# A decoder block's MLP weights: steps of the first up units and of the second down chunk held back and pinned in order, the last sums of up laid between the first down products

## The chip, the cores and the metric

The kernel runs on one core of a Trainium2 chip. The metric is the device time of one execution in microseconds (us). TensorE is called PE below, VectorE DVE, ScalarE ACT, GpSimd POOL and SyncE SP, as the profile does.

## What is computed

A decoder block on a sequence of 1024 rows of 1024 numbers: two token mixers (dilated attention and retention) behind one input projection, an output projection with a residual add, and an MLP. The change touches the last two steps:

```python
x = x + y @ w_out[l]
xn2 = rmsnorm(x, norm2_g[l])
x = x + jnp.square(jax.nn.relu(xn2 @ w_up[l])) @ w_down[l]
```

`w_up` is 1024 x 4096, `w_down` 4096 x 1024, all in float32.

## The kernel before

**Products.** Every float32 operand is split into a high half (`h`, a rounded copy made by ACT, line 320) and a low half (`l`, the rest, a subtraction on DVE, line 321). A product is three matmuls: high by high, high by low, low by high. The matmuls stand in `Pipe.group`, line 223. The large projections, up and down among them, are done by a scheme with seven products in place of eight, named N1 to N7. For it sums and differences of weight quarters are made first.

**Weights.** The class `Weights` holds a list of steps. A step takes a weight quarter that SP has loaded into a buffer `raw`, makes a sum on DVE where the scheme needs one (line 121 for the units of up, line 153 for the chunks of down), and splits it. Steps run strictly in the order of the list. `pump` runs as many as can run: those whose place is free and whose raw buffers can be loaded. It is called whenever a place comes free, and loads the next raw buffers behind each step, so a step that is issued later also sends its loads to SP's queue later. For up a unit (16 of them) has the pieces A, D, B and C; the list starts A of unit 0, A of unit 1, then D, B and C of unit 0, and so on. For down a chunk (8 of them) has seven steps, N1, N2, N3, N5, N7, N6, N4, of which the last four need a sum. Chunks use two sets of places in turn; some of the second set's lie in buffers that only come free when up ends (`n2a`, `n3a`, `y1a`, `w1a` and others).

**Order of the instructions.** PE's order is as written. On the other engines a scheduler may move an instruction ahead of others by its own estimate of when the inputs are there. `keep_in_program_order(ins)` pins one instruction behind everything that was recorded before it on its engine.

**The end of the output projection, place one below.** For each of eight row tiles `t` DVE adds the residual (`xr`, line 1148), ACT squares it, DVE and POOL make the inverse root (`ssq`, lines 1152 and 333, 334), and DVE scales the two halves of the row (`xn2`, line 1156). PE transposes the result into a PSUM tile `tr` (line 1092; there are two such tiles), and `turn_xn` makes the operands of up from it: `x0`, `x2`, `x3` and, last, `x1` (line 1112), each with a split. The line 1112 row is the last reader of its `tr` tile.

**The end of up and the start of down, place two.** `result` squares the ReLU of up's products (`u3`, `u2`, `q11`, `q12`), makes four sums `s` from each unit (line 1197) and sends all of it to memory (`h_d`). Down reads its rows back from there (`load_rows`), splits them (`part_rows`: ACT line 1245, POOL line 1246), and runs its products `down(u, name)`, where a unit `u` is a chunk and one of four row tiles. The result of a product is added into the output rows `Y` by DVE (line 1279) or copied there by ACT (line 1277); N1 is copied by ACT with its sign turned (`ms`, line 1271). Two products of unit 0 run inside up's last unit, the others behind it.

Of the kernel before, what the change touches and what calls it, by code (L numbers as in the profile page):

```python
# [10 lines left out]
F = mybir.dt.float32  # L11
R = mybir.dt.float32r
AF = mybir.ActivationFunctionType
# [4 lines left out]
P = 128  # L18
# [19 lines left out]
class Weights:  # L38
# [12 lines left out]
    def __init__(self, nc, rawp, wp, split):  # L51
# [8 lines left out]

        self.places = {}

    def claim(self, buf, key):
# [31 lines left out]
    def add_units(self, tag, srcs):  # L95

        base = len(self.src)
        kept = {}
        for s in srcs:
# [3 lines left out]
        def piece(key, buf, r, cols, then=None):  # L103
            def step():
# [4 lines left out]
                else:  # L109
                    h, l = self.buffer(buf)  # L110
                self.split(h, l, self.raw[r][:, cols])
                self.units[key] = h, l
# [5 lines left out]
        def sums(r):  # L118
            (x22, x21), (x11, x12) = ((self.raw[i][:, 0:512], self.raw[i][:, 512:1024]) for i in (r, r + 1))
            for x, y in ((x22, x21), (x21, x11), (x11, x22), (x12, x11)):  # L120
                self.nc.vector.tensor_tensor(x, x, y, op=OP.add)

# [14 lines left out]
    def add_chunks(self, tag, srcs, buffers):  # L137


        for c, quarters in enumerate(srcs):  # L140
# [4 lines left out]
            for name, r, other, op, ends in (  # L145
# [4 lines left out]

                def step(r=r, other=other, op=op, ends=ends, buf=buf, key=key):
                    if other is not None:
                        self.nc.vector.tensor_tensor(self.raw[r], self.raw[r], self.raw[other], op=op)  # L153
                    h, l = self.buffer(buf)
                    self.split(h, l, self.raw[r])
                    self.units[key] = h, l
                    self.used.update(ends)
# [22 lines left out]
    def pump(self, most=99):  # L180
        while most > 0 and self.next < len(self.steps):
            before, r, step = self.steps[self.next]
# [69 lines left out]

DOWN = ("N6", "N5", "N7", "N3", "N4", "N1", "N2")
BANK = {"N1": "a", "N2": "a", "N6": "b", "N7": "b", "N4": "b", "N5": "d", "N3": "d"}

# [14 lines left out]
def hybrid_block(ctx: ExitStack, tc: tile.TileContext, a: dict, out: bass.AP):  # L270
# [47 lines left out]

    def split(dst_h, dst_l, src):
        nc.scalar.activation(dst_h, src, AF.Copy)  # L320
        nc.vector.tensor_tensor(dst_l, src, dst_h.bitcast(F), op=OP.subtract)  # L321
# [16 lines left out]


    W = Weights(nc, rawp, wp, split)  # L340
    heads = [(slot, g) for slot in range(SLOTS) for g in (1, 2, 0)]
    for slot, g in heads:
# [733 lines left out]
    with ExitStack() as ph:  # L1076
# [10 lines left out]
        def turn_xn(xn, t, q):  # L1087
# [25 lines left out]
            put(OP7["N4"], cut, x1)  # L1113

        order = [(0, t) for t in range(NT)] + [(1, t) for t in (0, 4, 1, 5, 2, 3, 6, 7)]
        ahead = []
# [14 lines left out]
        for nb in range(2):  # L1131
            us = W.take(4)
            ns = halves()[nb]
            for n, t in enumerate([t for b, t in order if b == nb]):
# [16 lines left out]
                if nb == 1:  # L1151
# [3 lines left out]
                    for q, (cs, x2) in enumerate(zip(halves(), (y0, y))):  # L1155
                        nc.vector.scalar_tensor_tensor(xn[:, cs], x2, ssq[:, t, 3:4], g2[:, cs],
                                                       op0=OP.mult, op1=OP.mult)
                        pipe.at(2 if n > 5 else 1, lambda xn=xn, t=t, q=q: turn_xn(xn, t, q))

    last_turn = max(pipe.due)  # L1160


    with ExitStack() as ph:
# [16 lines left out]
        def result(j, f, cs, src):  # L1180
# [19 lines left out]
        held = {}  # L1200

# [115 lines left out]
        W.free(("place", "y1"))  # L1317
        load_rows(3)


    with ExitStack() as ph:
# [117 lines left out]
```

## Time and profile before

| | |
|---|---|
| median of 3 runs | 2254.57 us (2253.41 to 2255.34) |
| profiled execution | 2252.05 us |
| its span | 2250.3 us |
| PE busy | 2211.8 us (98%) |
| DVE busy | 1351.1 us (60%) |
| ACT busy | 1047.8 us (47%) |
| POOL busy | 398.6 us (18%) |
| granted PE clock, mean | 0.998 |

A row of a timeline in the profile gives the start and the duration of one instruction in us, the engine, the line, the operation with its output and inputs and, in brackets, how long the engine had stood idle before it and what ended that. A row on weight halves has the line of the helper `split`, so it is told from others by its tile: `wh` and `wl` are weights, `xh` and `xl` operands (or weights that lie in an operand's buffer). Matmuls follow each other before the one in front has ended, so durations of neighbours overlap. The profile is of one execution; its matmul ends are modelled.

### The profile page before, as it was taken

Reading aid. Unit: us, or ns where it says so; the run is one execution under the profiler, and the core shown is the slowest. Engines: PE = TensorE matmul, PEld = TensorE weight load, DVE = VectorE, ACT = ScalarE, POOL = GpSimd, SP = SyncE. Lnnn points to the kernel's source line nnn. Section 1 sums busy time; section 2 is a strip of 40 time slices with the busy share of each in tenths; the row PEclk is TensorE's granted clock in tenths of the full one; section 3 lists DMA queues with packets and bytes.
Section 4 is the critical chain, followed back from the end, with each engine's and each line's share of the span. In section 5 each row is a group of like instructions: output and inputs, shape, how many; then the busy total and the mean of one; then the engine's idle time right before and its main releaser. Section 6 shows DMA issues by size and latency. Waiting matters only on the chain. (4 is left out here: it accounts for less than half of the span.)

```text
span 2250.3 us, 30678 instructions
## 1 busy us (share of the span) xinstructions
PE 2211.8 (98%) x10772; PEld 1893.1 (84%) x10772; DVE 1351.1 (60%) x2570; ACT 1047.8 (47%) x2352; POOL 398.6 (18%) x436
## 2 busy tenths in 40 slices
PE   8999999999999999999999999999999999899999
PEld 7999999998888888888888877787788888678787
DVE  6444545454644445557777767783855556777874
ACT  6444434445343333445555544442555555654542
POOL 1111111110000000001222130000000000587873
PEclk9999999999999999999999999999999999999999
DMA  4313222322233333253563477774244456644432
GB/s 150 99 50 102 72 83 86 104 86 94 71 113 113 113 113 113 103 175 102 151 193 112 127 244 266 264 240 160 102 140 150 150 152 203 222 149 172 174 126 103
DMA packets 247852, 311.64 MB, mean 138 GB/s; under 512 B 15377, under 2 KB 171409, under 8 KB 247698
## 3 DMA queue, kind: packets, MB, share of 16 engines
q1 hardware_dynamic: 247698, 309.69, 42.5%
q8 instruction: 84, 1.38, 0.2%
q14 instruction: 70, 0.57, 0.1%
HBM read 209.92 MB, written 99.71 MB: 138 GB/s over the span
## 5 line engine op out<-in xcount | busy, mean ns | idle before, releaser
L321 DVE TENSOR_TENSOR wl<-raw,wh 128x1024 fp32r<-128x1024 f32 (+2 forms) x290 | 317.4, 1097 | 366.5 <-ACT wh L320 365.4
L223 PE MATMUL mm<-wh,xh 128*128 128x384 f32 (+1 forms) x1226 | 482.0, 393 | 1.8 <-ACT xh L320 1.3
L223 PE MATMUL mm<-wh,xl 128*128 128x384 f32 (+1 forms) x1226 | 439.1, 358 | 2.3 <-DVE xl L321 2.2
L320 ACT ACTIVATE wh<-raw 128x1024 fp32r<-128x1024 f32 (+2 forms) x290 | 273.5, 945 | 360.3 <-PE ms L223 110.8
L223 PE MATMUL mm<-wl,xh 128*128 128x384 f32 (+1 forms) x1226 | 437.6, 357 | 0.0
L223 PE MATMUL mm<-xh,wh 128*128 128x512 f32 x720 | 281.6, 391 | 5.0 <-ACT ms L387 5.0
L223 PE MATMUL mm<-xl,wh 128*128 128x512 f32 x720 | 280.7, 390 | 1.7 <-DVE xl L321 1.7
L223 PE MATMUL mm<-xh,wl 128*128 128x512 f32 x720 | 280.7, 390 | 0.0
L223 PE MATMUL ms<-xh,wh 128*128 128x512 f32 x700 | 275.6, 394 | 1.9 <-DVE St L886 1.6
L223 PE MATMUL ms<-xl,wh 128*128 128x512 f32 x700 | 272.6, 389 | 0.0
L223 PE MATMUL ms<-xh,wl 128*128 128x512 f32 x700 | 272.5, 389 | 0.0
L223 PEld LDWEIGHTS mm<-wh,xl 128*128 128x128 f32 x1226 | 230.7, 188 | 23.0 <-DVE xl L321 3.7
L223 PEld LDWEIGHTS mm<-wh,xh 128*128 128x128 f32 x1226 | 231.8, 189 | 21.6 <-ACT xh L320 1.7
L223 PEld LDWEIGHTS mm<-wl,xh 128*128 128x128 f32 x1226 | 232.6, 190 | 16.7
L223 PEld LDWEIGHTS mm<-xh,wh 128*128 128x128 f32 x720 | 135.6, 188 | 35.1 <-ACT ms L387 7.1
L223 PEld LDWEIGHTS mm<-xl,wh 128*128 128x128 f32 x720 | 135.5, 188 | 30.1 <-DVE xl L321 2.1
L223 PEld LDWEIGHTS mm<-xh,wl 128*128 128x128 f32 x720 | 135.5, 188 | 28.1
L223 PEld LDWEIGHTS ms<-xh,wh 128*128 128x128 f32 x700 | 131.5, 188 | 30.3 <-DVE St L886 2.0
L223 PEld LDWEIGHTS ms<-xh,wl 128*128 128x128 f32 x700 | 131.4, 188 | 27.4
L223 PEld LDWEIGHTS ms<-xl,wh 128*128 128x128 f32 x700 | 131.5, 188 | 26.3
L334 POOL TENSOR_TENSOR ssa<-ssa,half 128x2 f32<-128x2 f32 x96 | 66.5, 693 | 427.3 <-DVE ssa L333 410.3
L872 POOL TENSOR_TENSOR st<-st,half 128x1 f32<-128x1 f32 x32 | 27.5, 858 | 645.3 <-DVE st L871 645.2
(300 smaller groups left out, 3663.6 us busy)
## 6 DMA issues: line engine op xcount, KB each, us to landing
raw<-in_w_att SPq DMA_DIRECT2D x48, 384.0 KB, 3.9
raw<-in_w_up SPq DMA_DIRECT2D x32, 512.0 KB, 4.0
h_d<-s SPq DMA_DIRECT2D x64, 256.0 KB, 4.5
raw<-in_w_down SPq DMA_DIRECT2D x32, 512.0 KB, 4.4
s<-sg_d SPq DMA_DIRECT2D x40, 256.0 KB, 4.0
xh<-h_d SPq DMA_DIRECT2D x11, 896.0 KB, 4.5
s<-on_d SPq DMA_DIRECT2D x36, 256.0 KB, 5.0
xl<-h_d SPq DMA_DIRECT2D x10, 896.0 KB, 4.7
```

Of the source, the lines that this page charges most:

```text
L223: self.nc.tensor.matmul(ps, x, y, start=start, stop=stop, skip_group_check=not first)
L320: nc.scalar.activation(dst_h, src, AF.Copy)
L321: nc.vector.tensor_tensor(dst_l, src, dst_h.bitcast(F), op=OP.subtract)
L334: nc.gpsimd.tensor_tensor(dst, dst, half[:, :w], op=OP.pow)
L872: nc.gpsimd.tensor_tensor(st[:, 9:10], st[:, 8:9], half[:, 0:1], op=OP.pow)
```

## The change

Four edits. The first holds back the list of weight steps: a `limit` stops `pump` behind the first two steps of up while the output projection runs, and behind the first chunk of down while up runs; each limit is lifted later (the first behind the output projection, the second when the first down unit is issued). The second pins the sums and the high halves (ACT's copies) of the held-back steps, D, B and C of up's units 0 and 1 and the whole second chunk of down, behind what was recorded before them. The third records the four last sums `s` of up one by one (`add_tail`), the last unit's pinned and laid between the first seven down products. The fourth takes these seven products out of the last loop and records them ahead of it, so that the second chunk's steps come behind them in the program. No arithmetic or transfer is added or removed, and PE's order stays as it was.

```diff
     def pump(self, most=99):
-        while most > 0 and self.next < len(self.steps):
+        while most > 0 and self.next < len(self.steps) and self.next != self.limit:
...
-                self.split(h, l, self.raw[r][:, cols])
+                self.split(h, l, self.raw[r][:, cols], key[0] == "up" and key[1] < 2 and key[2] != "A")
...
-                self.nc.vector.tensor_tensor(x, x, y, op=OP.add)
+                ins = self.nc.vector.tensor_tensor(x, x, y, op=OP.add)
+                if tag == "up" and r <= base + 2:
+                    self.keep(ins)
...
-                def step(r=r, other=other, op=op, ends=ends, buf=buf, key=key):
+                def step(r=r, other=other, op=op, ends=ends, buf=buf, key=key, pin=c == 1):
                     if other is not None:
-                        self.nc.vector.tensor_tensor(self.raw[r], self.raw[r], self.raw[other], op=op)
+                        ins = self.nc.vector.tensor_tensor(self.raw[r], self.raw[r], self.raw[other], op=op)
+                        if pin:
+                            self.keep(ins)
                     h, l = self.buffer(buf)
-                    self.split(h, l, self.raw[r])
+                    self.split(h, l, self.raw[r], pin)
...
+DOWN_ORDER = (("N6", False), ("N5", False), ("N1", True), ("N7", False), ("N2", True), ("N3", False), ("N4", False))
...
-    def split(dst_h, dst_l, src):
-        nc.scalar.activation(dst_h, src, AF.Copy)
+    def split(dst_h, dst_l, src, pin=False):
+        hi = nc.scalar.activation(dst_h, src, AF.Copy)
+        if pin:
+            tc.keep_in_program_order(hi)
         nc.vector.tensor_tensor(dst_l, src, dst_h.bitcast(F), op=OP.subtract)
...
+        W.limit = W.first["up"] + 2
         order = [(0, t) for t in range(NT)] + [(1, t) for t in (0, 4, 1, 5, 2, 3, 6, 7)]
...
+    W.limit = None
+    W.pump()
     last_turn = max(pipe.due)
...
                 for name, x, y in (("N5", "u3", "u2"), ("N7", "u2", "q11"), ("N6", "q11", "N5"), ("N3", "q12", "N6")):
-                    held[j, name] = temps().tile([P, 512], F, name="s", bufs=4)
-                    nc.vector.tensor_tensor(held[j, name], held[j, x], held[j, y], op=OP.add)
-                    put_operand(j, name, held[j, name])
+                    tail.append((j, name, x, y))
+                    if j < NU - 1:
+                        add_tail()
...
+        def add_tail():
+
+            j, name, x, y = tail.pop(0)
+            held[j, name] = temps().tile([P, 512], F, name="s", bufs=4)
+            ins = nc.vector.tensor_tensor(held[j, name], held[j, x], held[j, y], op=OP.add)
+            if j == NU - 1:
+                tc.keep_in_program_order(ins)
+            put_operand(j, name, held[j, name])
...
+        W.limit = len(W.steps) - 7 * (NC - 1)
         stream = [(0, "N1"), (0, "N2")]
...
         W.free(("place", "y1"))
         load_rows(3)
+        for name, later in DOWN_ORDER:
+            down(later, name)
+            if name in ("N2", "N3", "N4"):
+                add_tail()
+        add_tail()
+        W.limit = None
...
-        for u in range(len(units)):
-            for name, later in (("N6", False), ("N5", False), ("N1", True), ("N7", False), ("N2", True),
-                                ("N3", False), ("N4", False)):
+        for u in range(1, len(units)):
+            for name, later in DOWN_ORDER:
```

Place one, DVE, in the kernel before: the norm of a row tile (`xr`, `ssq`, `xn2`) with the D pieces and the sums of up's units between its rows.

```order
L1148 TENSOR_TENSOR xr_15176<-mm_15244,xr_15176 128x512
L321 TENSOR_TENSOR wl4_15304<-raw0_14883,wh4_15303 128x512
L1152 TENSOR_TENSOR ssq_14655<-ssq_14655 128x1
L121 TENSOR_TENSOR raw0_14883<-raw0_14883 128x512
L333 TENSOR_SCALAR ssq_14655<-ssq_14655 128x1
L321 TENSOR_TENSOR wl4_15304<-raw2_14897,wh4_15303 128x512
L1156 SCALAR_TENSOR_TENSOR xn2_15293<-y0_15178,ssq_14655,g2_14653 128x512
L1156 SCALAR_TENSOR_TENSOR xn2_15293<-xr_15176,ssq_14655,g2_14653 128x512
L121 TENSOR_TENSOR raw0_14883<-raw0_14883,raw1_14895 128x512
L321 TENSOR_TENSOR xl_97<-x0_15319,xh_96 128x4x128
L121 TENSOR_TENSOR raw1_14895<-raw1_14895,raw0_14883 128x512
```

The same stretch of DVE in the changed kernel: from the row behind the same residual add to the first held-back row.

```order
L1163 TENSOR_TENSOR ssq_14655<-ssq_14655 128x1
L342 TENSOR_SCALAR ssq_14655<-ssq_14655 128x1
L1167 SCALAR_TENSOR_TENSOR xn2_15293<-y0_15178,ssq_14655,g2_14653 128x512
L1167 SCALAR_TENSOR_TENSOR xn2_15293<-xr_15176,ssq_14655,g2_14653 128x512
L330 TENSOR_TENSOR xl_97<-x0_15311,xh_96 128x4x128
L330 TENSOR_TENSOR xl_99<-x1_15329,xh_98 128x4x128
L1159 TENSOR_TENSOR xr_15240<-mm_15296,xr_15240 128x512
L1163 TENSOR_TENSOR ssq_14655<-ssq_14655 128x1
L342 TENSOR_SCALAR ssq_14655<-ssq_14655 128x1
L1167 SCALAR_TENSOR_TENSOR xn2_15345<-y0_15242,ssq_14655,g2_14653 128x512
L1167 SCALAR_TENSOR_TENSOR xn2_15345<-xr_15240,ssq_14655,g2_14653 128x512
L330 TENSOR_TENSOR wl4_15349<-raw0_14883,wh4_15348 128x512
```

The two norms now stand without weight rows between theirs; the first held-back row, `wl4`, comes behind the second.

Further on DVE, in the kernel before: from the first split of row tile 6's second half to its `x1` row.

```order
L321 TENSOR_TENSOR xl_93<-tr_15401,xh_92 128x4x128
L1107 TENSOR_TENSOR x2_15395<-x2_15395,tr_15401 128x512
L1108 TENSOR_TENSOR tr_15401<-x0_15259,tr_15401 128x512
L321 TENSOR_TENSOR xl_95<-x0_15259,xh_94 128x4x128
L321 TENSOR_TENSOR xl_13058<-x2_15395,xh_13057 128x4x128
L321 TENSOR_TENSOR xl_13062<-tr_15401,xh_13061 128x4x128
L1112 TENSOR_TENSOR x1_15277<-x1_15277,tr_15401 128x512
```

And in the changed kernel, from the first sums of unit 0 to the same `x1` row.

```order
L1113 TENSOR_TENSOR x0_15259<-x0_15259,tr_15390 128x512
L123 TENSOR_TENSOR raw1_14895<-raw1_14895,raw0_14883 128x512
L330 TENSOR_TENSOR xl_93<-tr_15401,xh_92 128x4x128
L123 TENSOR_TENSOR raw1_14895<-raw1_14895 128x512
L1117 TENSOR_TENSOR x2_15395<-x2_15395,tr_15401 128x512
L1118 TENSOR_TENSOR tr_15401<-x0_15259,tr_15401 128x512
L330 TENSOR_TENSOR wl2_15357<-raw1_14895,wh2_15356 128x1024
L330 TENSOR_TENSOR wl5_15361<-raw0_14883,wh5_15360 128x1024
L330 TENSOR_TENSOR xl_13062<-tr_15401,xh_13061 128x4x128
L330 TENSOR_TENSOR xl_95<-x0_15259,xh_94 128x4x128
L330 TENSOR_TENSOR xl_13058<-x2_15395,xh_13057 128x4x128
L1122 TENSOR_TENSOR x1_15277<-x1_15277,tr_15401 128x512
```

The sums and the two low halves of 1024 (pieces B and C of unit 0, `wl2` and `wl5`) now stand ahead of the `x1` row's last three splits; before, they stood ahead of the whole piece.

Place two, DVE, in the kernel before: from the first low half of the second chunk (`y1al`) to the eviction of unit 0's N7 (`Y4` with `ms`). `xl_93` is a weight's place here.

```order
L153 TENSOR_TENSOR raw0_17674<-raw0_17674,raw3_17710 128x1024
L401 TENSOR_TENSOR u2_17625<-mm_17627,u2_17625 128x512
L321 TENSOR_TENSOR xl_93<-raw2_17708,xh_92 128x1024
L321 TENSOR_TENSOR wl3_17769<-raw0_17674,wh3_17768 128x1024
L153 TENSOR_TENSOR raw3_17710<-raw3_17710,raw2_17708 128x1024
L1197 TENSOR_TENSOR s_17736<-u3_17663,u2_17625 128x512
L1197 TENSOR_TENSOR s_17739<-u2_17625,q11_17552 128x512
L1197 TENSOR_TENSOR s_17742<-q11_17552,s_17736 128x512
L321 TENSOR_TENSOR xl_93<-raw1_17706,xh_92 128x1024
L1197 TENSOR_TENSOR s_17745<-q12_17697,s_17742 128x512
L153 TENSOR_TENSOR raw2_17708<-raw2_17708,raw0_17674 128x1024
L1279 TENSOR_TENSOR Y4_15468<-Y4_15468,ms_17683 128x512
```

And in the changed kernel, from the last subtraction of up on.

```order
L411 TENSOR_TENSOR u2_17625<-mm_17627,u2_17625 128x512
L1302 TENSOR_TENSOR Y4_15468<-Y4_15468,ms_17683 128x512
L1219 TENSOR_TENSOR s_17798<-u3_17663,u2_17625 128x512
L1302 TENSOR_TENSOR Y0_15467<-Y0_15467,mm_17761 128x512
L1219 TENSOR_TENSOR s_17811<-u2_17625,q11_17552 128x512
L1219 TENSOR_TENSOR s_17823<-q11_17552,s_17798 128x512
L1219 TENSOR_TENSOR s_17826<-q12_17697,s_17823 128x512
L330 TENSOR_TENSOR y1al_17744<-raw0_17674,y1ah_17743 128x1024
L330 TENSOR_TENSOR xl_93<-raw1_17706,xh_92 128x1024
L330 TENSOR_TENSOR xl_93<-raw2_17708,xh_92 128x1024
L157 TENSOR_TENSOR raw0_17674<-raw0_17674,raw3_17710 128x1024
L1302 TENSOR_TENSOR Y5_17741<-Y5_17741,ms_17778 128x512
```

The eviction of N7 moved from behind the second chunk's first three low halves, three of its sums and all `s` to the row behind `u2`; the `s` rows stand next to it, and the second chunk behind them.

Place two, ACT, in the kernel before: the copies of the second chunk's last three steps and the eviction of unit 2's N1 (`ms`) behind them.

```order
L1277 ACTIVATE Y4_15468<-ms_17683 128x512
L1245 ACTIVATE xh_94<-r2_17754 128x256
L1277 ACTIVATE Y1_17752<-ms_17831 128x512
L320 ACTIVATE w1ah_17777<-raw3_17710 128x1024
L320 ACTIVATE w1bh_17779<-raw2_17708 128x1024
L320 ACTIVATE w1ch_17781<-raw1_17706 128x1024
L1277 ACTIVATE Y5_17753<-mm_17881 128x512
L1271 ACTIVATE ms_17898<-mm_17891 128x512
```

And in the changed kernel, where the same copies stand further on.

```order
L1300 ACTIVATE Y5_17741<-ms_17778 128x512
L327 ACTIVATE w1ah_17833<-raw3_17710 128x1024
L1300 ACTIVATE Y2_17747<-ms_17898 128x512
L1268 ACTIVATE xh_94<-xh_96 128x256 x2
L1300 ACTIVATE Y6_17748<-mm_17948 128x512
L1268 ACTIVATE xh_94<-xh_96 128x256
L327 ACTIVATE w1bh_17835<-raw2_17708 128x1024
L1294 ACTIVATE ms_17965<-mm_17958 128x512
```

The copy `w1bh`, pinned, now stands right in front of the eviction of unit 3's N1, with other evictions and row splits between the copies.

More of the change, by code (lines that the diff above doesn't have):

```diff
@@ L61, in __init__ @@
         self.places = {}
+        self.limit, self.keep, self.first = None, None, {}
     def claim(self, buf, key):
@@ L97, in add_units @@
         base = len(self.src)
+        self.first[tag] = len(self.steps)
         kept = {}
@@ L340, in hybrid_block @@
     W = Weights(nc, rawp, wp, split)
+    W.keep = tc.keep_in_program_order
     heads = [(slot, g) for slot in range(SLOTS) for g in (1, 2, 0)]
@@ L1195, in result @@
                 for name, x, y in (("N5", "u3", "u2"), ("N7", "u2", "q11"), ("N6", "q11", "N5"), ("N3", "q12", "N6")):
-                    held[j, name] = temps().tile([P, 512], F, name="s", bufs=4)
-                    nc.vector.tensor_tensor(held[j, name], held[j, x], held[j, y], op=OP.add)
-                    put_operand(j, name, held[j, name])
-        held = {}
+                    tail.append((j, name, x, y))
+                    if j < NU - 1:
+                        add_tail()
+        held, tail = {}, []
+        def add_tail():
[5 more added lines that the diff above has]
+            put_operand(j, name, held[j, name])
         def put_operand(j, name, x):
```

## The prediction

> **What bounds the kernel now.** I read the page first, then the waits of TensorE (PE), then a table of 25 us windows, then the timelines of the two windows in which PE loses most. The page:
>
> ```profile
> span 2250.3 us, 30678 instructions
> PE 2211.8 (98%) x10772; PEld 1893.1 (84%) x10772; DVE 1351.1 (60%) x2570; ACT 1047.8 (47%) x2352; POOL 398.6 (18%) x436
> ```
>
> PE is busy for 2211.8 of 2250.3 us, so 38.5 us is all that an edit can win which leaves its matmuls alone. The waits of PE from 1500 us on (line waited for: total, times, longest) and the windows (span, then busy time of PE, PEld, DVE, ACT, POOL, then the granted clock) show where the share of these two places lies:
>
> ```profile
> PE ms L223 <- DVE Y L1279: 5.8, 2, 5.0
> PE tr L1092 <- DVE x L1112: 2.8, 1, 2.8
> PE mm L223 <- ACT ms L1271: 1.4, 2, 0.9
> 1600.00:1625.00 25.00, 21.12 (x105) 16.57 (x103) 23.78 (x43) 15.92 (x29) 2.40 (x3) 1.00 0.30 101
> 1625.00:1650.00 25.00, 24.09 (x102) 20.01 (x103) 15.73 (x23) 15.32 (x25) 0.00 (x0) 0.93 0.28 84
> 1925.00:1950.00 25.00, 18.99 (x75) 14.58 (x74) 17.85 (x18) 15.91 (x29) 11.28 (x10) 0.93 0.80 277
> 1950.00:1975.00 25.00, 24.45 (x108) 19.93 (x107) 15.31 (x15) 18.55 (x38) 17.95 (x18) 1.00 0.40 139
> ```
>
> Place one is the start of up (1600 to 1630 us): VectorE (DVE) is busy for 23.78 of 25 us and PE waits for it. Place two is the end of up and the start of down (1930 to 1955 us). At both the granted clock averages 0.93 for a window: 0.07 x 25 = 1.75 us lost once more in each. PE at place one, and behind it PE at place two (start, duration, what, idle before):
>
> ```profile
> 1614.14 0.50 PE L223 MATMUL mm<-xl,wh 128*128 128x512 f32 x1 [1.73 <-DVE xl L321]
> 1622.69 0.40 PE L223 MATMUL mm<-xh,wl 128*128 128x512 f32 x1
> 1625.90 1.06 PE L1092 MATMUL tr<-ident,xn 128*128 128x128 f32 x4 [2.82 <-DVE x L1112]
> 1627.19 0.63 PE L223 MATMUL mm<-xl,wh 128*128 128x512 f32 x1
> 1629.58 0.39 PE L223 MATMUL mm<-xl,wh 128*128 128x512 f32 x1
> ...
> 1933.66 0.50 PE L223 MATMUL ms<-xh 128*128 128x512 f32 x1 [0.86 <-ACT Y L1277]
> 1938.11 0.39 PE L223 MATMUL mm<-wh,xl 128*128 128x512 f32 x1
> 1943.52 0.79 PE L223 MATMUL ms<-wh,xh 128*128 128x512 f32 x1 [5.02 <-DVE Y L1279]
> 1952.69 0.50 PE L223 MATMUL mm<-wh,rh 128*128 128x512 f32 x1 [0.55 <-ACT ms L1271]
> ```
>
> Behind each long wait the matmuls take 0.63 us in place of 0.39; at place one that ends by 1629.58, some 3.4 us after the wait. The wait of 5.02 us is for an eviction, Y -= PSUM of the first down unit's N7, which DVE does only at 1942.79 (row below). N7 started at 1933.66 and its six matmuls, 0.23 us apart, were done by about 1935.3: DVE was 7.5 us late, with weight steps of the second chunk in front.
>
> **Place one, step by step.** DVE's rows, by which the new order is added up:
>
> ```profile
> 1594.18 0.68 DVE L1148 TENSOR_TENSOR xr<-mm,xr 128x512 f32<-128x512 f32 x1
> 1596.66 0.75 DVE L1156 SCALAR_TENSOR_TENSOR xn<-y,ssq,g 128x512 f32<-128x512 f32 x1 [0.66 <-POOL ssq L334]
> 1598.00 0.68 DVE L1103 TENSOR_TENSOR x<-x,tr 128x512 f32<-128x512 f32 x1
> 1608.13 0.69 DVE L1148 TENSOR_TENSOR xr<-mm,xr 128x512 f32<-128x512 f32 x1
> 1615.81 1.22 DVE L321 TENSOR_TENSOR wl<-raw,wh 128x1024 fp32r<-128x1024 f32 x1
> 1616.94 0.69 DVE L1148 TENSOR_TENSOR xr<-mm,xr 128x512 f32<-128x512 f32 x1
> 1624.48 0.68 DVE L321 TENSOR_TENSOR xl<-tr,xh 128x512 fp32r<-128x512 f32 x1
> 1625.08 0.67 DVE L1112 TENSOR_TENSOR x<-x,tr 128x512 f32<-128x512 f32 x1
> 1649.08 0.69 DVE L121 TENSOR_TENSOR raw<-raw 128x512 f32<-128x512 f32 x1
> 1649.81 0.69 DVE L121 TENSOR_TENSOR raw<-raw,raw 128x512 f32<-128x512 f32 x1
> ```
>
> A 512-wide row starts 0.60 us after the one before it (1624.48 to 1625.08), a 1024-wide one takes 1.13 (1615.81 to 1616.94), a sum that waits for its predecessor 0.73 (1649.08 to 1649.81). A row norm with nothing else in it costs DVE 3.82 us, from the residual add at 1594.18 to 1598.00, of which it waits some 1.4 us for ACT and for GpSimd (POOL). In the kernel before, the last two norms (from 1608.13 and 1616.94) have weight rows laid into these holes. In the changed order the weight rows stand behind the last norm, so the holes are empty.
>
> From the common row at 1608.13 to the end of the L1112 row that PE waits for, the new order is: a norm 3.82, two low halves 1.20, a norm 3.82, which is 1616.97; then a D half and the first two sums, 0.73 + 0.73 + 0.60 to the next row; six rows of 512 (two of them sums) 3.60; two weight low halves of 1024 that now stand in front, 2.26; three low halves 1.80; the row itself 0.67. That ends at 1627.4, against 1625.08 + 0.67 = 1625.75: **+1.6 us**. The wait of 1.73 at 1614.14 shrinks, since the low half that ends it has one or two weight rows fewer ahead, but PE then only stands earlier at the 2.82 wait, which grows to about 6. It is worth nothing: DVE sets the end. A bound below is that DVE hides half of the holes (0.2 us later than before); above, that ACT's pinned copies hold DVE up by one copy more (+2.7).
>
> The slow clock goes the other way. If the slow stretch stands in time as it did (1625.9 to 1629.3), PE runs only 1.9 us of it and loses 0.9 in place of 1.75: **-0.8 us** (from 0 to -1.75). Last, the third 1024-wide weight row stands between the last rows' low halves, and the first N6 product needs one of those: up to one such row, 0 to 1.13, taken as **+0.6**. Place one: +1.6 - 0.8 + 0.6 = +1.4 us.
>
> [...]
>
> **Place two.** In the new order the N7 eviction stands right behind the u2 subtraction of the last up unit, ahead of all seven chunk-two splits and four sums; the last four up sums stand between the evictions. Waits of 0.86 and 5.02, the slow stretch of 1.75 and the 0.55 go: -8.2 us. What is late next are the held-back steps themselves, which now fall on the first down products:
>
> ```profile
> 1930.29 1.23 DVE L153 TENSOR_TENSOR raw<-raw,raw 128x1024 f32<-128x1024 f32 x1
> 1940.62 2.83 POOL L1246 TENSOR_TENSOR xl<-r,xh 128x256 fp32r<-128x256 f32 x2
> 1941.13 1.74 DVE L153 TENSOR_TENSOR raw<-raw,raw 128x1024 f32<-128x1024 f32 x1
> 1942.79 0.68 DVE L1279 TENSOR_TENSOR Y<-Y,ms 128x512 f32<-128x512 f32 x1
> 1946.61 0.73 POOL L1246 TENSOR_TENSOR xl<-r,xh 128x256 fp32r<-128x256 f32 x1 [3.16 <-ACT xh L1245]
> 1948.72 1.05 ACT L320 ACTIVATE w1ah<-raw 128x1024 fp32r<-128x1024 f32 x1
> 1952.05 0.59 ACT L1271 ACTIVATE ms<-mm 128x512 f32<-128x512 f32 x1
> raw<-in_w_down SPq DMA_DIRECT2D x32, 512.0 KB, 4.4
> ```
>
> For the weights themselves there is room. Eleven DVE rows at 1.74 are 19.1 us from about 1940 on, and their products (unit 4 on, three units of seven products of 1.36 us, six matmuls 0.23 us apart, behind unit 0) begin some 28 us after it. But ACT's queue is in order, and the pinned copies stand in it ahead of N1 evictions (L1271) on which PE waits for a PSUM bank. The copy w1bh waits for a sum that DVE makes behind another split: between 0 and one slowed sum and its copy, 1.74 + 1.05 = 2.8; I take 1.6, near to the slowed sum, since POOL is at work there. A copy of chunk three waits for its transfer, issued later than before because SP holds it behind DVE's pinned rows: between 0 and a whole landing of 4.4; I take 1.4, a third of it. With 0.2 for N1's eviction of unit 1 the new waits are **+3.2**, and place two is -8.2 + 3.2 = -5.0 us. No wait of these is over 2 us, so no slow stretch is counted.
>
> The same row shows two prices: 1.23 alone, 1.74 with POOL at work, and two POOL rows take 2.83 beside it where one takes 0.73 alone. [...] It speaks against the change, which moves eleven such rows to where POOL works; the sum has them at 1.74 already.
>
> **The sum.** The profiled execution took 2252.05 us (its span and 1.75 around it): 2252.05 + 1.4 - 5.0 = 2248.45. That execution lies 2.52 under the median of the runs, 2254.57; the same -3.6 from there gives **2251.0 us**, 0.16% less. About 0.2%, 4.5 us, is what a measurement of this kernel can tell from no change, so this counts as the same. With the new waits of place two between 0 and 2.8 + 4.4 its own range is 2248 to 2255.
>
> **Rivals.** First, the new waits do not come: ACT has its sums and landings in time, since DVE is busy for only 15.31 of 25 us from 1950 us on. Then -3.6 - 3.0 = -6.6, 2248.0, faster. For it: ACT is busy for 18.55 of 25 us at most here. Against: 0.55 of such a wait is there already.
>
> Second, slower: ACT is held at each of its seven pinned copies by a slowed sum, with an eviction behind each: 7 x 1.74 = 12.2 in place of 3.0, so -3.6 + 9.2 = +5.6, 2260.2. It decides from the point where more than half of the copies, about 6.6 us of holding, keep PE. Against it: three of the seven need no sum.
>
> [...]
>
> Fourth, the change does not do what it says: the N7 eviction stays late because ACT hands it over late. Place two then gains nothing and place one stands: +1.4, 2256.0.
>
> **Chances.** Forecast 0.55, first rival 0.22, second 0.06, third 0.13, fourth 0.04. Faster by over 0.2% (under 2250.1): the first and 0.06 of the forecast's own spread, 0.28. Slower by over 0.2%: the second and 0.02 of others, 0.08. The same: 0.64. The range, 2247.3 to 2256.0, reaches from the first rival to the fourth and leaves out the second.
>
> **What would show it.** Right: at place one PE's wait for the L1112 row (its new line) is 5 to 6.5 us, and the wait for xl before it under 1; at place two no wait for Y over 1 us, the clock at 1.00, and two waits of 1 to 2 us for the N1 eviction within 30 us. Wrong: a wait for L1112 under 4 us (the holes were filled after all), a wait for Y over 2 us, or ACT waits of over 4 us in all.

## The result and the profile after

The changed kernel took 2251.28 us (median of 22 runs, 2249.09 to 2254.3) beside 2254.66 of the kernel before: a ratio of 0.9986, 95% interval 0.9979 to 0.9992, so 3.2 us less (1.8 to 4.7). The forecast was 2251.0 and -3.6. Its profiled execution, however, took 2252.3 us, no less than the 2252.05 of the profile before. The page of the kernel after, span and busy times:

```profile
span 2250.5 us, 30672 instructions
PE 2212.8 (98%) x10772; PEld 1892.7 (84%) x10772; DVE 1352.6 (60%) x2570; ACT 1047.7 (47%) x2352; POOL 398.7 (18%) x436
```

The waits of TensorE (PE) from 1500 us on in the kernel after (line waited for: total, times, longest; L1122 and L1302 are the old L1112 and L1279, L1294 the old L1271):

```profile
PE tr L1102 <- DVE x L1122: 5.9, 1, 5.9
PE mm L229 <- ACT ms L1294: 4.1, 3, 1.9
PE ms L229 <- DVE Y L1302: 0.7, 1, 0.7
PE mm L229 <- DVE xl L330: 0.6, 2, 0.3
```

At the start of up the wait of 2.8 us has become one of 5.9, and the one of 1.73 ahead of it is down to 0.3; at the start of down the 5.0 us wait for Y is gone, and of the three waits for the N1 eviction two are new. The 25 us windows of the kernel after (span, then busy time of PE, PEld, DVE, ACT, POOL, then the granted clock):

```profile
1600.00:1625.00 25.00, 22.37 (x110) 17.57 (x108) 20.85 (x38) 15.30 (x28) 2.03 (x3) 1.00 0.21 73
1625.00:1650.00 25.00, 21.25 (x87) 17.60 (x88) 17.86 (x26) 14.57 (x25) 0.00 (x0) 0.86 0.31 91
1925.00:1950.00 25.00, 24.93 (x109) 20.27 (x110) 15.98 (x17) 17.76 (x35) 13.33 (x15) 1.00 0.82 270
1950.00:1975.00 25.00, 21.55 (x86) 16.74 (x85) 20.83 (x18) 17.20 (x33) 19.71 (x17) 0.93 0.50 170
```

DVE is now idle for 4 of 25 us in the window in which it sets the end (20.85, before 23.78): the empty holes of the norms. The clock reads 0.86 at place one (before 0.93), and the 0.93 of place two has moved from the first of its windows to the second. PE's timeline after, place one and place two (start, duration, what, idle before):

```profile
1613.90 0.50 PE L229 MATMUL mm<-xl,wh 128*128 128x512 f32 x1 [0.27 <-DVE xl L330]
1628.75 1.09 PE L1102 MATMUL tr<-ident,xn 128*128 128x128 f32 x4 [5.86 <-DVE x L1122]
1630.06 0.63 PE L229 MATMUL mm<-xl,wh 128*128 128x512 f32 x1
1633.30 0.39 PE L229 MATMUL mm<-xh,wh 128*128 128x512 f32 x1
...
1958.47 0.50 PE L229 MATMUL mm<-wh,rh 128*128 128x512 f32 x1 [1.55 <-ACT ms L1294]
1970.48 0.50 PE L229 MATMUL mm<-xh 128*128 128x512 f32 x1 [1.86 <-ACT ms L1294]
1971.52 0.63 PE L229 MATMUL mm<-xh 128*128 128x512 f32 x1
1982.63 0.50 PE L229 MATMUL mm<-xh 128*128 128x512 f32 x1 [0.73 <-ACT ms L1294]
```

The matmuls of 0.63 us are those at half clock. The wait of 1.86 us brought them on as well. The clock record of the traces gives the half-clock stretches as 3.413 us long (from 1625.94 and from 1943.38 us in the kernel before, from 1970.99 us in the kernel after) or twice that (6.827 us from 1626.25 us in the kernel after); 3.41 us is called a window of the clock below.

Where the time went is read from the same four matmuls in both traces, one ahead of and one behind each place (PE does the same matmuls in the same order in both). In the kernel before:

```profile
1590.07 0.39 PE L223 MATMUL mm<-wl,xh 128*128 128x512 f32 x1
1640.01 0.39 PE L223 MATMUL ms<-xh,wl 128*128 128x512 f32 x1
1925.17 0.39 PE L223 MATMUL mm<-wh,rh 128*128 128x512 f32 x1
1990.06 0.39 PE L223 MATMUL mm<-y1ah,xh 128*128 128x512 f32 x1
```

and in the kernel after:

```profile
1591.28 0.39 PE L229 MATMUL mm<-wl,xh 128*128 128x512 f32 x1
1643.29 0.39 PE L229 MATMUL ms<-xh,wl 128*128 128x512 f32 x1
1928.52 0.39 PE L229 MATMUL mm<-wh,rh 128*128 128x512 f32 x1
1990.24 0.39 PE L229 MATMUL mm<-y1ah,xh 128*128 128x512 f32 x1
```

Place one took 52.01 us in place of 49.94: +2.1. Place two took 61.72 in place of 64.89: -3.2. The 1.2 us ahead of 1591 lie ahead of the rows that the change moves. In six profiles of the experiments that leave place one as it was, the same stretch reads -0.5 to +5.4 us, so it is scatter between executions. With it the profile comes out even. The rest of the difference between profile and timed runs is the clock. The granted clock is listed for every run: its mean is 0.99720 over the 65 runs of the kernel before beside the experiments and 0.99764 over the 22 of the kernel after. Times the span of 2250 us that is 6.3 and 5.3 us lost. The two profiled executions lost 4.3 (half of 3.41 + 3.41 + 1.71 us at half clock, the last of them behind the last matmul) and 5.9 (half of 6.83 + 3.41 + 1.65). By this the profile before was lucky by 2.0 us and that after unlucky by 0.6, which is 2.6 of the 3.6 us by which the difference of the profiles (+0.25) and that of the medians (-3.4) disagree. It is an estimate that takes all clock lost for time lost, which after_fill below shows not to hold at place one.

### The profile page after: what moved, and what is told of

Same layout as the page of the kernel before. It is cut to its first block, busy times and chain, and to the rows that moved or that the text cites. A ratio compares the mean times of both kernels' runs of the same rounds, so it can differ in the third digit from the quotient of the medians.

```text
span 2250.5 us, 30672 instructions
## 1 busy us (share of the span) xinstructions
PE 2212.8 (98%) x10772; PEld 1892.7 (84%) x10772; DVE 1352.6 (60%) x2570; ACT 1047.7 (47%) x2352; POOL 398.7 (18%) x436
## 3 DMA queue, kind: packets, MB, share of 16 engines
q8 instruction: 84, 1.38, 0.2%
```

## The experiments

The table has, for every kernel, place one and place two against the kernel before, read from the same four matmuls; the stretches at half clock in each (us); and the ratio of the timed runs to those of the kernel before on the same chip, with its interval and in us of 2254.57. The readings of a place scatter: place two is unchanged in p1_only and p1_hold and reads -0.6 and +0.9, and p2_nopin and nopin_again are the same kernel.

| kernel | place one | place two | half clock one / two | ratio (95%) | us |
|---|---|---|---|---|---|
| changed kernel | +2.1 | -3.2 | 6.83 / 3.41 | 0.9986 (0.9979 to 0.9992) | -3.2 |
| p1_only | +1.9 | -0.6 | 6.83 / 3.41 | 1.0013 (1.0004 to 1.0022) | +2.9 |
| p2_only | -0.3 | -4.6 | 0 / 0 | 0.9976 (0.9966 to 0.9987) | -5.4 |
| p2_spread | -0.3 | -5.1 | 0 / 0 | 0.9970 (0.9960 to 0.9981) | -6.8 |
| after_fill | +1.7 | -2.1 | 0 / 3.41 | 0.9989 (0.9980 to 0.9998) | -2.5 |
| p1_hold | +0.3 | +0.9 | 0 / 6.83 | 0.9994 (0.9985 to 1.0003) | -1.4 |
| p2_nopin | -0.3 | -6.4 | 0 / 0 | 0.9962 (0.9948 to 0.9975) | -8.6 |
| p2_nosums | 0.0 | -4.2 | 3.41 / 0 | 0.9974 (0.9964 to 0.9985) | -5.9 |
| p2_late | 0.0 | -4.6 | 3.41 / 3.41 | 0.9968 (0.9956 to 0.9981) | -7.2 |
| pool_a | +1.9 | -6.2 | 6.83 / 0 | 0.9966 (0.9954 to 0.9978) | -7.7 |
| pool_b | +8.0 | -6.2 | 13.65 / 0 | 0.9998 (0.9990 to 1.0007) | -0.5 |
| pool_c | +5.8 | -6.6 | 10.24 / 0 | 0.9987 (0.9977 to 0.9996) | -2.9 |
| nopin_again | 0.0 | -6.8 | 3.41 / 0 | 0.9962 (0.9949 to 0.9974) | -8.6 |

**The two places apart.** p1_only has the edits of the start of up alone, p2_only those of the end of up and the start of down alone.

```diff
 p1_only, from the changed kernel
-    def step(..., key=key, pin=c == 1):
+    def step(..., key=key, pin=False):
...
-                    if j < NU - 1:
-                        add_tail()
+                    add_tail()
...
-            if j == NU - 1:
-                tc.keep_in_program_order(ins)
...
-        W.limit = len(W.steps) - 7 * (NC - 1)
...
-        for name, later in DOWN_ORDER:
-            down(later, name)
...
-        for u in range(1, len(units)):
+        for u in range(len(units)):
 p2_only, from the changed kernel
-        W.limit = W.first["up"] + 2
...
-                if tag == "up" and r <= base + 2:
-                    self.keep(ins)
-                self.split(h, l, self.raw[r][:, cols], key[0] == "up" and ...)
+                self.split(h, l, self.raw[r][:, cols])
```

> Place one alone: the hold and the pins at the start of up stay, the end of up and the start of down are as before the change. By the terms of the forecast: 1.4 us slower than the kernel before (1.6 of DVE order, 0.8 of slow clock less, 0.6 of wait for xl). By what the profile after the change shows, where TensorE stands 2.1 us later behind place one and the slow clock lasts for 6.83 us in place of 3.41: 2.1 us slower, and the wait for the L1122 row about 5.9 us again. Rival: the difference upstream of up (1.2 us in the profile at 1550 us) belongs to the change: 3.3 us slower.

> Place two alone: the start of up is as before the change, the weight steps of the second down chunk are held back and pinned and the last sums of up laid between the first down products. By the terms of the forecast: 5.0 us faster than the kernel before. By what the profile after the change shows (3.2 us won between 1890 and 1990 us, since a wait of 1.86 us brought a slow stretch of 3.41 us): 3.2 us faster. Rival: the two places are not independent, since place one shifts the phase at which the clock windows fall: then this and place one alone don't add up to the whole (0.9986 of the time before, 3.4 us).

PE's timeline in p1_only: the wait for L1122 is that of the changed kernel, and the long wait for Y of the kernel before is back (4.19 us, there 5.02).

```profile
1628.29 1.09 PE L1102 MATMUL tr<-ident,xn 128*128 128x128 f32 x4 [5.90 <-DVE x L1122]
1945.70 0.50 PE L229 MATMUL ms<-wh,xh 128*128 128x512 f32 x1 [4.19 <-DVE Y L1298]
```

PE's timeline in p2_only: the two waits for the N1 eviction.

```profile
1958.56 0.50 PE L227 MATMUL mm<-wh,rh 128*128 128x512 f32 x1 [1.54 <-ACT ms L1291]
1970.25 0.50 PE L227 MATMUL mm<-xh 128*128 128x512 f32 x1 [1.53 <-ACT ms L1291]
```

Place one alone costs 2.9 us (0.9 to 5.0), an interval that holds the 1.4, the 2.1 and the 3.3 of its expectation (the profile reads +1.9 at the place), and place two alone gains 5.4 (2.9 to 7.7); their sum, -2.5, is that of the whole (-3.2, 1.8 to 4.7) within the intervals. The changed kernel is a gain and a loss, as forecast. In p2_only the two waits, 1.54 and 1.53, brought no slow stretch, and place two gained 4.6 in place of 3.2.

**Is it the clock or DVE that costs at place one?** after_fill keeps PE busy through the long wait.

```diff
 after_fill, from the changed kernel
+        self.ps = ps
...
-    const.tile([P, 224], F, name="rest")
+    zero = const.tile([P, 224], R, name="rest")
+    nc.gpsimd.memset(zero.bitcast(F), 0.0)
...
             pt = tr.tile([P, 4, P], F, name="tr")
+            if (q, t) == (1, NT - 1):
+                for _ in range(48):
+                    nc.tensor.matmul(pipe.ps[:, :224], zero[:, :P], zero, start=False, stop=False, ...)
```

> The changed kernel, with 48 products of zeros (128x224, some 0.1 us each, 4.8 us in all) added into the open sum just ahead of the transposes that wait 5.86 us at place one; the result of the sum is unchanged. TensorE is then idle for about 1 us in place of 5.86, and the transposes start when they did. If the slow clock behind the wait is brought by the idle time and costs what its stretch of 6.83 us in the profile says, this is up to 3.4 us faster than the changed kernel; if it is one window in most runs, 1.7 us faster. Rival: the slow stretch hides beside DVE's work, which stays the bound behind place one: no difference, or slower by what the fill overruns.

PE's timeline in after_fill:

```profile
1623.70 5.51 PE L1104 MATMUL mm<-rest 128*128 128x224 f32 x48
1629.77 0.63 PE L1107 MATMUL tr<-ident,xn 128*128 128x128 f32 x4 [0.56 <-DVE x L1127]
1634.32 0.50 PE L230 MATMUL ms<-xh,wh 128*128 128x512 f32 x1 [0.48 <-ACT xh L328]
1635.42 0.51 PE L230 MATMUL ms<-xl,wh 128*128 128x512 f32 x1 [0.60 <-DVE xl L331]
```

The fill took the idle time and the slow stretch away (transposes of 0.63 us in place of 1.09, clock 1.00), and the time did not move: 0.9989 against 0.9986, each with runs of the kernel before beside it. By the two intervals the fill won some 1.8 us at most, which excludes the 3.4 and leaves one window's 1.7 at the edge. PE gained speed until 1634 and then waited 0.48 and 0.60 us for the operands of N6, which the changed kernel does not wait for there. So at place one the whole slow stretch of 6.83 us is worth 0.4 us (+1.7 in place of +2.1), not 3.4: it lies beside DVE's and ACT's next rows. The kernels without the change at place one say the same: with one slow stretch of 3.41 us they take 0.0 there, without one -0.3. PE in p2_only, p2_spread and p2_nopin, which have none, waits 0.67 us for an xl near 1633 us, and does not in p2_late, p2_nosums and nopin_again, which have one. The rival held.

**Hold or pins, at place one.** p1_hold keeps the limit and drops the pins.

```diff
 p1_hold, from p1_only
-                if tag == "up" and r <= base + 2:
-                    self.keep(ins)
-                self.split(h, l, self.raw[r][:, cols], key[0] == "up" and ...)
+                self.split(h, l, self.raw[r][:, cols])
```

> Place one alone, with the hold of the first two up units' steps, but without the pins on their sums and copies; place two as before the change. If the pins make the 2 us of place one, since without them the scheduler lays the weight rows into the holes of the last norms again, this is within 0.7 us of the kernel before, and the wait for the L1122 row is 3 us or less. If the hold itself makes them: 2 us slower than before, with a wait near 5.9 us.

PE's timeline in p1_hold:

```profile
1627.92 0.63 PE L1100 MATMUL tr<-ident,xn 128*128 128x128 f32 x4 [2.94 <-DVE x L1120]
```

The wait is 2.94 again and the time that of before (0.9994). Without pins the scheduler lays the weight rows into the holes again, and the hold by itself costs little: the place reads +0.3 with no slow stretch, where kernels with neither hold nor slow stretch read -0.3. The pins make the rest of the 1.9 us of p1_only.

**The parts of place two.** p2_nopin drops the pins on the held steps, p2_nosums the laying of the four sums.

```diff
 p2_nopin, from p2_only
-    def step(..., key=key, pin=c == 1):
+    def step(..., key=key, pin=False):
 p2_nosums, from p2_only
-                    if j < NU - 1:
-                        add_tail()
+                    add_tail()
...
-            if j == NU - 1:
-                tc.keep_in_program_order(ins)
...
-            if name in ("N2", "N3", "N4"):
-                add_tail()
-        add_tail()
```

> Place two alone, with the hold and the last four sums laid between the first down products, but without the pins on the second chunk's copies and sums. If the pins are what keeps VectorE free for the N7 eviction, the weight steps stand ahead of it again, a wait of 3 to 5 us for Y comes back and the gain falls from 5.4 to 2 us or less. If the hold and the sums do it: 5 us faster than before as with the pins, and the two waits for the N1 eviction (1.54 and 1.53 us) go, since the copies need not stand in front of it.

> Place two alone, with the hold and the pins, but the last four sums of up made at once, as before the change. If the laying of the sums matters, four sums of 0.7 to 1.0 us stand ahead of the evictions of the first down unit: a wait of 1 to 3 us for Y comes back, and this is 1 to 3 us slower than place two alone. Rival: within 0.5 us of place two alone, since the held-back weight steps were all the delay.

> p2_nopin again, as it was, beside the three variants on the same chip. It should come out at 0.9962 of the time before again, within 0.0013, if the gain over place two with pins (0.9976) is real; if that was the phase of the slow clock, at 0.997 to 0.998.

PE's timeline in p2_nopin, then ACT's:

```profile
1937.36 0.50 PE L227 MATMUL ms<-xh 128*128 128x512 f32 x1 [0.79 <-ACT Y L1297]
1940.59 0.50 PE L227 MATMUL mm<-wh,xh 128*128 128x512 f32 x1 [1.58 <-ACT ms L1291]
```

```profile
1949.24 0.58 ACT L1291 ACTIVATE ms<-mm 128x512 f32<-128x512 f32 x1
1950.60 1.04 ACT L325 ACTIVATE w1ah<-raw 128x1024 fp32r<-128x1024 f32 x1
1951.55 1.04 ACT L325 ACTIVATE w1bh<-raw 128x1024 fp32r<-128x1024 f32 x1
1952.50 1.04 ACT L325 ACTIVATE w1ch<-raw 128x1024 fp32r<-128x1024 f32 x1
```

Without pins no wait for Y came back. The three copies into w1 now stand in a row behind the N1 eviction of unit 2, none of them waiting, and the waits ahead of the N1 evictions of units 3 and 4 are gone. Left are 0.79 and 1.58 at the very start of down, the latter for unit 1's N1, and 0.87 us near 1980, which the kernel before has too. Place two gains 6.4 and 6.8 us in two profiles against 4.6 with pins, and the ratio is 0.9962 twice against 0.9976. The intervals of the ratios still overlap (0.9948 to 0.9975 and 0.9966 to 0.9987), so the 3 us between them are likely rather than certain. It has the lowest ratio of the study, though the intervals of p2_late and pool_a overlap with its own. p2_nosums is as fast as p2_only (0.9974 and 0.9976; no wait for Y over 0.3 us): the laying of the sums is worth nothing measurable. What p2_nopin and p2_nosums share is the hold, with the first unit's products recorded ahead of the held steps, and this is the likeliest to clear the way for the evictions. It is not shown alone: no run drops the pins and the laying together, or has one of these two edits without the other.

**Releasing the steps one at a time.** p2_spread releases one step behind each product of the second unit, p2_late the last three of them two to four products later.

```diff
 p2_spread, from p2_only
-        W.limit = len(W.steps) - 7 * (NC - 1)
+        HELD = W.limit = len(W.steps) - 7 * (NC - 1)
...
-        W.limit = None
...
                     down(u + later, name)
+                    if u < 3 and W.limit is not None and W.limit < HELD + 7:
+                        W.limit += 1
+                        W.pump()
...
 p2_late, the same with a table
+RELEASE = {(1, "N6"): 1, (1, "N5"): 1, (1, "N1"): 1, (1, "N7"): 1, (1, "N4"): 1, (2, "N1"): 1, (2, "N7"): 1}
```

> Place two alone, and the seven steps of the second down chunk released one behind each product of the second down unit, in place of all at once behind the first unit. If the two waits for the N1 eviction (1.55 and 1.86 us after the change) come from the pinned copies that stand in front of it in ACT's queue, they shrink to under 0.5 us each and no slow stretch follows: 3 to 5 us faster than place two alone. Rival: the waits are only moved, since chunk three's transfers are then issued later still: within 1 us of place two alone, with a wait of 1 to 2 us elsewhere between 1950 and 1990 us.

> Place two alone, the steps released one at a time as in p2_spread, but the last three later: one behind the second unit's N4, one behind the third unit's N1 and one behind its N7, so that the copy w1bh stands behind the N1 eviction that waited for it. If the order of ACT's queue makes the wait that is left (1.59 us), it goes and this is 1 to 1.5 us faster than p2_spread. Rival: VectorE's sums and splits of these steps, at 1.7 us each beside GpSimd, now stand ahead of Y evictions two units later, or chunk three's transfers come later: as p2_spread or up to 2 us slower, with the waits for Y (1.03 and 0.65 us) longer.

PE's timeline in p2_spread:

```profile
1957.29 0.50 PE L227 MATMUL mm<-wh,rh 128*128 128x512 f32 x1 [1.59 <-ACT ms L1291]
1961.34 0.50 PE L227 MATMUL ms<-wh,rh 128*128 128x512 f32 x1 [1.03 <-DVE Y L1299]
```

PE's and ACT's timelines in p2_late:

```profile
1966.29 0.61 PE L227 MATMUL mm<-xh 128*128 128x512 f32 x1 [2.39 <-ACT ms L1292]
```

```profile
1964.70 1.06 ACT L326 ACTIVATE xh<-raw 128x1024 fp32r<-128x1024 f32 x1 [1.41 <-DVE raw L155]
1965.66 0.58 ACT L1292 ACTIVATE ms<-mm 128x512 f32<-128x512 f32 x1
```

Both rivals were nearer. In p2_spread the wait for the N1 eviction of unit 4 went, that of unit 3 stayed at 1.59, and a wait for Y of 1.03 came; in p2_late the 1.59 went and one of 2.39 came, behind a third-chunk copy that waits for a sum which DVE makes late, behind the moved splits. The time over place two hardly moves (-5.1 and -4.6 beside -4.6), and the ratios (0.9970, 0.9968 and 0.9976) lie within each other's intervals: where the steps are released moves the wait, and no gain of it can be told from the scatter.

**Moving rows of place one to the idle GpSimd (POOL).**

```diff
 pool_a, from p2_nopin (pool_b: the same for N1 and N2 of the first four tiles; pool_c: both)
+            (low or nc.vector).tensor_tensor(l, src, h.bitcast(F), op=OP.subtract)
...
-            put(OP7["N5"], cut, x3)
-            put(OP7["N7"], cut, x2)
+            put(OP7["N5"], cut, x3, nc.gpsimd)
+            put(OP7["N7"], cut, x2, nc.gpsimd)
```

> p2_nopin, and at place one the low halves of N5 and N7 of the last four row tiles (8 rows of 128x512) are made by GpSimd in place of VectorE. If VectorE is the bound at place one, 8 x 0.60 = 4.8 us fewer of its work between 1600 and 1630 us shortens the waits of 1.7 and 2.8 us there: 1 to 3 us faster than p2_nopin. Rival: GpSimd, with 0.73 us for a row of 256 and so some 1.5 for one of 512, slows VectorE's own rows beside it (1.23 to 1.74 us): no difference, or up to 2 us slower, and the N5 and N7 products wait for GpSimd.

> p2_nopin, and at place one the low halves of N1 and N2 of the first four row tiles (8 rows of 128x512) are made by GpSimd in place of VectorE. These stand earlier, so that the last chain gains less: 0.5 to 2 us faster than p2_nopin if VectorE is the bound, no difference or slower by up to 1 us if its rows run slower beside GpSimd, since the first products of up wait for N1.

> Both moves of pool_a and pool_b: 16 rows on GpSimd. [...]

The longest wait of PE from 1580 to 1700 us in pool_b, and POOL's and DVE's rows around a norm in it:

```profile
PE tr L1102 <- DVE xn L1166: 5.7, 2, 5.4
```

```profile
1609.31 1.30 POOL L1095 TENSOR_TENSOR xl<-x,xh 128x512 fp32r<-128x512 f32 x1 [7.81 <-ACT xh L1094]
1610.57 0.55 POOL L341 TENSOR_TENSOR ssq<-ssq,half 128x1 f32<-128x1 f32 x1
```

```profile
1611.15 1.77 DVE L1166 SCALAR_TENSOR_TENSOR xn<-y,ssq,g 128x512 f32<-128x512 f32 x1 [1.77 <-POOL ssq L341]
```

The author's estimate for pool_c, both moves together, was 1.5 to 4 us faster than p2_nopin if the gains add up, and slower than either if 16 rows of some 1.5 us on GpSimd become the bound.

None gained; pool_c came out between the two (0.9987 beside 0.9966 and 0.9998). In pool_b a low half on POOL takes 1.30 us and stands in front of the power of the norm's sum of squares, which POOL makes too; the norm's first row then waits 1.77 us and runs at 1.77 in place of 0.75. In all three PE's longest wait became one for the norm (2.6, 5.4 and 6.3 us), and the wait for the L1122 row behind it is still 2.0 to 2.5 us. That DVE sets the end at place one is not refuted by this, but relieving it by POOL in these ways does not work.

## Why the prediction was right, and where it was not

**Place one, the order of DVE: right.** The forecast had the L1112 row end at 1627.4. DVE's rows after:

```profile
1614.36 0.68 DVE L1159 TENSOR_TENSOR xr<-mm,xr 128x512 f32<-128x512 f32 x1
1618.18 0.69 DVE L330 TENSOR_TENSOR wl<-raw,wh 128x512 fp32r<-128x512 f32 x1
1627.92 0.68 DVE L1122 TENSOR_TENSOR x<-x,tr 128x512 f32<-128x512 f32 x1
```

The row ended at 1628.60, less the 1.21 us that the program stood later already: 1627.39. The empty norm took 3.82 us (1614.36 to 1618.18), as counted, and PE's wait was 5.86 within 5 to 6.5.

**Place one, the slow clock: wrong.** The step "PE runs only 1.9 us of it ... -0.8 us" failed twice. The stretch lasted two windows, and after_fill shows that its length hardly matters there: 6.83 us are worth 0.4, one window 0.3. So the term was +0.1, not -0.8. The wait for xl, taken as +0.6, came out at 0.3: from the transposes to the matmul behind the place PE takes 14.15 us in after_fill and 13.82 in p2_only, neither with a slow stretch. The two make up the 0.43 us by which PE fell back there: it stood 2.85 us later than in the kernel before at the transposes (1628.75 against 1625.90) and 3.28 at the matmul behind the place (1643.29 against 1640.01). So +1.6 + 0.1 + 0.3 = +2.0 in place of +1.4; measured 2.1 and 1.9 in two profiles, 2.9 (0.9 to 5.0) in timed runs.

**Place two: the waits right, the clock mis-sized.** The waits of 0.86, 5.02 and 0.55 and the first slow stretch went. The two new waits have the causes that the forecast gave them, a copy behind a slowed sum and one of chunk three behind its transfer. ACT's rows after, each right in front of the N1 eviction that PE waits for:

```profile
1956.88 1.06 ACT L327 ACTIVATE w1bh<-raw 128x1024 fp32r<-128x1024 f32 x1 [1.02 <-DVE raw L157]
1968.89 1.06 ACT L327 ACTIVATE wh<-raw 128x1024 fp32r<-128x1024 f32 x1 [1.27 <-DMA raw<-in_w_down]
```

They were sized at 1.6 and 1.4 and measured at 1.55 and 1.86; the 0.2 for N1 of unit 1 did not come. That all eleven moved DVE rows take 1.74 us no run shows: in the profile after the four sums took 1.75 to 1.76 us, the seven low halves 1.21 to 1.25 (two of them 2.35 together). The third wait after, 0.73, stands in the kernel before as well:

```profile
1982.44 0.50 PE L223 MATMUL mm<-xh 128*128 128x512 f32 x1 [0.88 <-ACT ms L1271]
```

"No wait of these is over 2 us, so no slow stretch is counted" failed in the profiled execution: 1.86 us was enough. No run shows that bound of 2 us, which was the author's estimate; in the kernel before a wait of 1.73 us brought no stretch and one of 2.82 did. The slow stretch that was counted as won came back, and -5.0 became -3.2: -6.4 of waits gone, +3.4 of new ones, -0.2 on the third, 0 from the clock. It held in p2_only, whose waits were 1.54 and 1.53: -4.6 there, -5.4 timed.

**The rivals.** The first (new waits don't come) did not happen in this kernel; in p2_nopin those in front of units 3 and 4 are gone with the pins. The second and fourth did not happen. The third was that the slow stretches lie elsewhere in the timed runs than in the profile, which no run had shown then. It was right in this: waits of 2.8 to 2.9 us at place one brought a slow stretch in four profiles (the kernel before, p2_late, p2_nosums, nopin_again) and none in four others (p2_only, p2_spread, p2_nopin, p1_hold). In the traces the slow stretches begin at whole multiples of 3.413 us from one another (1625.94 and 1943.38 us in the kernel before, 93 of them apart), and where a stretch came went with how much of PE's idle time fell into one window of that grid. In the first four it was 2.1 to 2.8 us; in the others it was split, into 1.70 and 1.10 us in p2_nopin. The window of the wait in the kernel before and the one behind it, then the two that share the wait in p2_nopin (span, then busy time of PE, PEld, DVE, ACT, POOL, then the granted clock):

```profile
1622.53:1625.94 3.41, 0.59 (x4) 0.19 (x3) 3.41 (x7) 1.95 (x4) 0.00 (x0) 1.00 0.01 4
1625.94:1629.36 3.42, 3.42 (x11) 2.85 (x12) 3.35 (x6) 2.84 (x5) 0.00 (x0) 0.50 0.00 0
```

```profile
1624.30:1627.71 3.41, 1.71 (x10) 1.08 (x8) 3.41 (x7) 1.47 (x4) 0.00 (x0) 1.00 0.30 124
1627.71:1631.12 3.41, 2.31 (x12) 2.00 (x13) 3.41 (x7) 2.72 (x5) 0.00 (x0) 1.00 0.00 0
```

A wait of 5.02 us, split over two windows, leaves at least 2.51 us in one of them: waits of 5.02 and 5.03 us at place two brought one slow window in the kernel before and two in p1_hold. The price of 1.75 us for a stretch at place one was wrong too, since 6.83 us of it were worth 0.4 there. In the timed runs the clock did not eat the gain: the kernel before lost 6.3 us to it on average, the kernel after 5.3.

The median came out as forecast, 2251.28 beside 2251.0. That it lies this near is in part luck: the interval of the gain is 1.8 to 4.7 us, and the two places, forecast at +1.4 and -5.0, measured +2.1 and -3.2 in the profile and +2.9 and -5.4 each alone in timed runs.

**Left open.** Between the two places the kernels of place two alone (p2_only, p2_spread, p2_nopin, p2_nosums, p2_late, nopin_again) lose 0.5 to 1.4 us that neither the kernel before nor the changed one loses. In five of their six profiles 0.45 to 0.84 us of it is one wait of PE for an eviction near 1683 us; in p2_only a weight copy that waits for its transfer stands ahead of this eviction. Why it is late there was not tried.

## What to carry to other kernels

Where a scheduler fills an engine's holes, holding steps back and pinning them are two edits: here the gain at place two came with the hold, and the pins cost some 2 us at place one and probably as much at place two, so try each alone. Price a slow clock stretch by what runs beside it, not by half its length: where another engine sets the end, as DVE at place one, it is nearly free (6.83 us of it were worth 0.4). And compare a profiled execution with the granted clock of the timed runs before taking its time for the kernel's.

## What the runs showed of the hardware

- In each of the 14 traces all half-clock stretches begin at whole multiples of 3.413 us from one another (in the kernel before at 1625.94 and 1943.38 us, 93 of them apart; in the kernel after at 1626.25 and 1970.99 us, 101 apart). They went with what PE's idle time adds up to in one window of that grid, more than with the length of a single wait. Of the windows at full clock from 10 to 2235 us, all 17 with 1.92 us of idle time or more (2.82 and 3.41 in the kernel before, 3.36 in the kernel after) were followed by one at half clock, 6 of the 21 with 1.66 to 1.91 us (1.86 in the kernel after, but not 1.73 and 1.67 in the kernel before and 1.67 in the kernel after), and none with less. So p2_only's waits of 1.60 and 1.38 us near 1313 and 1524 us were followed by one each (1.71 and 1.72 us of idle time with the small gaps beside them), and one of 2.07 us near 1365 us in the kernel before, split, with 1.67 us in one window, by none.
- 48 small matmuls of zeros put into an open sum, 5.51 us in all, took the place of nearly all of a wait of nearly 6 us (0.56 us was left), and the granted clock read 1.00 in after_fill from 1600 to 1650 us, where the changed kernel has 0.86 from 1625 to 1650.
- A GpSimd low half of 128x512 took 1.26 to 1.30 us in seven rows of pool_a and pool_b, and up to 2.14 in others (pool_a). Two of them took 3.02 us in all beside two VectorE low halves of 128x512 that took 3.46, where such a row takes 0.69 (pool_b, from 1617.81 us). A VectorE row of two SBUF operands that met one ran at 1.77 us in place of 0.75 (pool_b); rows that read PSUM took 0.68 beside a GpSimd row in the kernel before (1931.43 and 1942.79 us).
- Beside a GpSimd row, the sum of 128x1024 at 1941.13 us in the kernel before took 1.74 us, but that at 1930.29 us, which the prediction reads as alone, kept 1.23 beside a GpSimd row of 1.73.
